# Sparse attention inside a two-layer trunk: which PSUM pool the value products use, where 1/8 is multiplied in, and when the last merge is transposed

## The chip, the cores and the metric

The kernel runs on one NeuronCore of one Trainium2 chip. The metric is the device time of one execution in microseconds (us), the median of three runs.

## What is computed

Two layers. Each is a half-step SwiGLU FFN, then a token-mixing block of three gated branches, then another half-step SwiGLU FFN, each with RMSNorm before and after and with shift, scale and gate from a conditioning vector. There are 256 tokens of width 1024. Only the second branch of the mixing block, the attention, is touched, and the step that merges the branches. The reference, cut to those:

```python
scale = HEAD_DIM ** -0.5                     # 1/8
def query_block(i):                          # 64 queries at a time; 8 heads in 2 groups
    ...
    s = jnp.einsum('bghqd,bgnd->bghqn', qn, kc)
    p_cmp = masked_softmax(s, cmp_end[None, :] <= t[:, None], scale)
    o_cmp = jnp.einsum('bghqn,bgnd->bghqd', p_cmp, vc)
    ...
    p = masked_softmax(s, m_slc, scale)      # selected keys (here: all causal ones)
    o_slc = ...
    p = masked_softmax(s, m_win, scale)      # window keys
    o_win = ...
    return gc[..., 0:1] * o_cmp + gc[..., 1:2] * o_slc + gc[..., 2:3] * o_win
...
branches = jnp.einsum('bsnw,nwd->bsnd', ys, w_branch)      # ys: gMLP, attention, conv
gates = jax.nn.sigmoid(h @ w_gate).reshape(Bsz, S, N_BRANCH, D_MODEL)
merged = jnp.einsum('bsnd,bsnd->bsd', gates, branches)
return merged @ w_out
```

## The kernel before

Every matrix product is done in three fp32r passes: a weight or an activation is split into a high part (`hi`, a copy on ScalarE) and the rest (`lo`, a subtraction on VectorE), and `mm3` (L169 to L172) issues hi by hi, hi by lo and lo by hi into one PSUM bank. Weights stream from HBM one megabyte at a time; `units` (L157) splits each into two such pairs (L164 on ScalarE, L165 on VectorE).

The tokens lie in two tiles of 128 (`t` = 0 and 1). PSUM has eight banks, dealt out by three pools: `ps_y` with four (`y_tile`), `ps_m` with two (`m_tile`) and `ps_t` with two (`t_tile`, for transposes). A tile takes a bank of its pool and gives it back after its last reader. The framework fixes the order of each engine's instructions when the kernel is built, from the order of the program text and from when it reckons each to be ready, and gives a tile its bank or buffer where that order has its first write. So the order on an engine is not quite that of the text.

In `mixing`, two streams of work are interwoven by hand. One is `bulk` (L511), a generator of the projections and branch products: one step is one `mm3` of 512 columns, eight steps make one token tile of a projection (`cg`, `xt`, `bg`, `v`, `u` and the gates `gt`), four steps one of a branch product (`br`). `chunk_steps` (L491) runs the two token tiles of one such product; it takes both banks from `ps_y` at its start and calls `evac` on each tile when its steps are done. The other stream is the attention: 16 pairs of token tile and head. For each, `scores` (L810) issues two products into an `m_tile` named `sc`, VectorE adds the causal mask (L816), takes the maximum (L818) and multiplies it by -1/8 (L819), ScalarE takes the exponential of both softmaxes with scale 1/8 and that bias (L822), and VectorE and ScalarE normalise (L823 to L826). `weights_t` (L829) transposes the result two heads later, and `values` (L856), for each pair of heads, multiplies with the values into another `m_tile`, named `pv`; its results go to the tiles `yTb` (L875 to L882; `yTb` and the pairs `pT`, `u`, `gp`, `ln`, the queries `qhT` and others share one SBUF pool of 14 buffers). The main loop (L885) calls `scores`, `weights_t` and `values` in turn and takes five or six steps of `bulk` after the first two.

The queries reach the scores through `query_hl` (L696): four transposes into one bank, then for each half of the partitions a high copy on ScalarE (L707) and a rest on VectorE (L708).

At the end, `down` (L927) runs the output product `yo`. For the second token tile it first finishes the last branch product (`rest`), whose result is added into `merged[1]` on VectorE (L606, L608); then `out_steps` does three of the eight k-steps (`OUT_AT = 3`), `merged_t(1, 1)` transposes the merged tile into `mT` (L907, L910, L911), and the other steps follow; those from the fifth on read that `mT`. `finish` (L315) puts the norm of the first token tile before this and the transposes of its result (`modulate`, L285) after it.

Of the kernel before, what the change touches and what calls it, by code (L numbers as in the profile page):

```python
# [9 lines left out]
F32 = mybir.dt.float32  # L10
F32R = mybir.dt.float32r
BF16 = mybir.dt.bfloat16
AF = mybir.ActivationFunctionType
ALU = mybir.AluOpType
AX = mybir.AxisListType
# [16 lines left out]
HOLD_CH = 4  # L32
HOLD_END = 2
OUT_END = 4
OUT_AT = 3
S4 = 14
F1 = 3
F2 = (5, 6)
# [36 lines left out]
def trunk(ctx: ExitStack, tc: tile.TileContext, order, x_in, c_in, wst, smalls, gmws, ng_rows, modb, lnrows, rope_c, mask_c, out):  # L75
# [9 lines left out]
    V, A, G, T = nc.vector, nc.scalar, nc.gpsimd, nc.tensor  # L85

    def s4(name, shape=(P, NT, 512), dt=F32):
        return sp.tile(list(shape), dt, name=name, tag="s4", bufs=S4)

    def s2(name, shape=(P, NT, 256), dt=F32):  # L90
        return sp.tile(list(shape), dt, name=name, tag="s2", bufs=S2)
# [4 lines left out]
    def sm(name, shape, bufs=4):  # L96
        return sp.tile(list(shape), F32, name=name, tag=name, bufs=bufs)

    def y_tile(name, n=2):
        return [ps_y.tile([P, 512], F32, name=name, tag="y") for _ in range(n)]  # L100

    def m_tile(name):
        return ps_m.tile([P, 512], F32, name=name, tag="m")

    def t_tile(name):
        return ps_t.tile([P, 512], F32, name=name, tag="t")
# [193 lines left out]
    def proj_steps(o, t, hT, us, width, kpu=2):  # L300
        n = len(us) * kpu
        for k in range(n):
            hi, lo = us[k // kpu]
            c = (k % kpu) * width
            ts = slice(t * P, (t + 1) * P)
            mm3(o, hT[0][:, k, ts], hT[1][:, k, ts], hi[:, c : c + width], lo[:, c : c + width], k == 0, k == n - 1)
            yield
# [179 lines left out]
    def mixing(l, hT, pend, nxt):  # L487
# [1 line left out]
            return units(("in", l, ((lo_c, n),), 0)) + units(("in", l, ((lo_c, n),), 1))  # L489

        def chunk_steps(evac, us, name, width=512, src=None, kpu=2, ts=range(NT)):  # L491
            for t, o in zip(ts, y_tile(name, len(ts))):
                yield from proj_steps(o[:, :width], t, src or hT, us, width, kpu)
                evac(t, o)

# [15 lines left out]
        def bulk():  # L511
            def run(us, name, evac, hooks, **kw):
                for k, _ in enumerate(chunk_steps(evac, us, name, **kw)):
                    if k in hooks:
                        hooks[k]()
                    yield
# [179 lines left out]
        def query_hl(t):  # L696


            o = s4("qhT", (P, 8, P), F32R)
            pt = t_tile("qht")  # L700
            for i in range(4):
                T.transpose(out=pt[:, i * P : (i + 1) * P], in_=qraw[:, t, 2 * i : 2 * i + 2].rearrange("p a d -> p (a d)"), identity=ident)
            pv = pt.rearrange("p (a q) -> p a q", a=4)
            ov = o.rearrange("p (a i) q -> p a i q", i=2)
            for i in range(2):
                r, s = slice(64 * i, 64 * i + 64), slice(64 - 64 * i, 128 - 64 * i)
                A.activation(ov[r, :, i], pv[r], AF.Copy)  # L707
                V.tensor_tensor(ov[s, :, i], pv[r], ov[r, :, i].bitcast(F32), ALU.subtract)  # L708
            return o

        vd = s4("vd", (P, NT, 4, 2, 64), F32R)
# [22 lines left out]
        fill(F1)  # L734
        key_t(kvc, 1)
        qhT = [query_hl(0), None]


# [31 lines left out]
        po = t_tile("po")  # L770
# [6 lines left out]
        po = t_tile("po")  # L777
# [32 lines left out]
        def scores(t, h):  # L810
            g, nk = h // 4, (t + 1) * P
            sc = m_tile("sc")[:, : 2 * nk].rearrange("p (b n) -> p b n", b=2)
            T.matmul(sc, lhsT=qhT[t][:, h], rhs=khv[:, :, g, :nk], start=True, stop=False)
            T.matmul(sc, lhsT=qhT[t][:, h], rhs=klv[:, :, g, :nk], start=False, stop=True)
            dg = sc[:, :, t * P : nk]
            V.tensor_tensor(dg, dg, mask[:, 0:128].unsqueeze(1).to_broadcast([P, 2, P]), ALU.add)  # L816
            mx, nsum = sm("mx", [P, 2]), sm("nsum", [P, 2])
            V.tensor_reduce(mx, sc, axis=AX.X, op=ALU.max)  # L818
            V.tensor_scalar(mx, mx, -0.125, None, op0=ALU.mult)  # L819
            pr = s2("pr", (P, 2, nk))  # L820
            for br in range(2):
                A.activation(pr[:, br], sc[:, br], AF.Exp, scale=0.125, bias=mx[:, br : br + 1], accum_out=nsum[:, br : br + 1])  # L822
            V.reciprocal(nsum, nsum)  # L823
            V.tensor_tensor(nsum, nsum, sg[:, t, h, 1:3], ALU.mult)
            V.tensor_scalar(pr[:, 0], pr[:, 0], nsum[:, 0:1], None, op0=ALU.mult)
            A.activation(pr[:, 1], pr[:, 1], AF.Copy, scale=nsum[:, 1:2])  # L826
            prs[t, h] = pr
# [28 lines left out]
        def values(t, hp):  # L856

            g, nb = hp // 2, t + 1
            po = m_tile("pv")[:, :256]
            hs = slice(2 * hp, 2 * hp + 2)  # L860
            pT = pTs.pop((t, hp))
            pairs = [(vc, [x[:, hs].rearrange("p h q -> p (h q)") for x in pcs[t]])]
            for n in range(2 * nb):
                br, kt = n // nb, n % nb
                pairs.append((vd[:, kt, 2 * br + g], [x[:, n].rearrange("p h q -> p (h q)") for x in pT]))
            for n, (v, (ph, pl)) in enumerate(pairs):
                if n > 0:
                    T.matmul(po[0:64], lhsT=v[:, 0], rhs=pl, start=False, stop=False)
                T.matmul(po, lhsT=v.rearrange("p a d -> p (a d)"), rhs=ph, start=n == 0, stop=n == 2 * nb)
                if n == 0:  # L870
                    T.matmul(po[0:64], lhsT=v[:, 0], rhs=pl, start=False, stop=False)
            ts = slice(t * P, (t + 1) * P)
            hi, lo = [x[:, hp, ts] for x in yT[1]]
            od = sm("od", [P, P], bufs=2)
            A.activation(hi[0:64], po[0:64, 0:P], AF.Copy)  # L875
            A.activation(od[64:128], po[0:64, P:256], AF.Copy)
            A.activation(od[0:64], po[64:128, 0:P], AF.Copy)
            A.activation(hi[64:128], od[64:128], AF.Copy)
            V.tensor_tensor(lo[0:64], po[0:64, 0:P], hi[0:64].bitcast(F32), ALU.subtract)
            V.tensor_tensor(lo[64:128], od[64:128], hi[64:128].bitcast(F32), ALU.subtract)  # L880
            V.tensor_tensor(lo[0:64], lo[0:64].bitcast(F32), od[0:64], ALU.add)
            V.tensor_tensor(lo[64:128], lo[64:128].bitcast(F32), po[64:128, P:256], ALU.add)  # L882

        heads = [(t, h) for t in range(NT) for h in range(8)]
        for i in range(len(heads) + 4):  # L885
            if i < len(heads):
                t, h = heads[i]
                scores(t, h)
                fill(F2[t])
                if h == 0:  # L890
                    cmp_t(t)
                if (t, h) == (0, 4):
                    qhT[1] = query_hl(1)
            if 0 <= i - LAG < len(heads):
                weights_t(*heads[i - LAG])
                fill(F2[heads[i - LAG][0]])
            j = i - LAG - 1
            if 0 <= j < len(heads) and heads[j][1] % 2 == 1:
                values(heads[j][0], heads[j][1] // 2)
# [4 lines left out]
        def merged_t(n, t):  # L904
            pt = t_tile("mt")
            for i in range(4):
                T.transpose(out=pt[:, i * P : (i + 1) * P], in_=merged[n][:, t, i * P : (i + 1) * P], identity=ident)  # L907
            pv = pt.rearrange("p (a b) -> p a b", a=4)
            hi, lo = [x[:, :, t * P : (t + 1) * P] for x in mT[n]]
            A.activation(hi, pv, AF.Copy, scale=0.5)  # L910
            V.scalar_tensor_tensor(out=lo, in0=pv, scalar=0.5, in1=hi.bitcast(F32), op0=ALU.mult, op1=ALU.subtract)  # L911
# [8 lines left out]
        def out_steps(t, ks):  # L920
            ts = slice(t * P, (t + 1) * P)
            for n, ns in enumerate(halves):
                for k in ks:
                    hi, lo = mT[k // 4]
                    mm3(y[t][n], hi[:, k % 4, ts], lo[:, k % 4, ts], wo[k][0][:, ns], wo[k][1][:, ns], k == 0, k == 7)

        def down(t, part):  # L927
# [5 lines left out]
            elif part == 0:  # L933
                for _ in rest[0]:
                    pass
                y[1] = y_tile("yo")
                out_steps(1, range(OUT_AT))
                merged_t(1, 1)
                out_steps(1, range(OUT_AT, 4))
                out_steps(1, range(4, OUT_END))  # L940
# [104 lines left out]
```

## Time and profile before

| | |
|---|---|
| median of 3 runs | 1291.8 us (1289.95 to 1295.27) |
| the profiled execution's own time | 1292.15 us |
| its span, first to last instruction | 1290.4 us |
| the two attention stretches in it | about 270 to 430 us and 901 to 1061 us |
| mean granted TensorE clock | 0.995 of full |

The span is one execution as the hardware profiler saw it. Each row of a timeline has a start in us, a duration, the engine, the line of the kernel, the operation and its tiles, and in brackets how long the engine had been idle and what ended that. Matmuls are pipelined: a row of 0.39 us is followed by the next after about 0.23 us, so rows overlap, and time lost between two matmuls is best read as the distance of their starts less the usual one.

### The profile page before, as it was taken

How to read it: one execution, taken by the hardware profiler on the slowest of the kernel's cores; microseconds unless marked ns; L12 is line 12 of the kernel's file. 1: busy time of each engine (PE TensorE's matmuls, PEld its weight loads, DVE VectorE, ACT ScalarE, POOL GpSimd, SP SyncE). 2: the span in 40 equal slices, each digit the busy share in tenths (PEclk: the TensorE clock that was granted, in tenths of full speed). 3: DMA queues.
4: the chain of work that ended last, by engine and by line, in shares of the span. 5: the costliest groups of instructions: out<-in, count | busy, mean ns of one | idle time of the engine just before them, and what ended most of it. 6: DMA issues, size and time to landing. Idle time of an engine off the chain costs nothing.

```text
span 1290.4 us, 15916 instructions
## 1 busy us (share of the span) xinstructions
PE 1254.8 (97%) x5922; PEld 1027.5 (80%) x5922; DVE 1028.6 (80%) x1632; ACT 680.9 (53%) x1129; POOL 31.6 (2%) x56
## 2 busy tenths in 40 slices
PE   6999999999999999999999999998999999999998
PEld 4788888778778878888878888887877887888886
DVE  7977997789999699767598767587999996875553
ACT  5454446476565464544465444456666574554442
POOL 1000001000000010000010000000000000100000
PEclk8999999999999999999999999999999999999999
DMA  8966885665466548767559767367535763684540
GB/s 328 362 234 248 325 325 193 228 236 186 173 264 238 224 180 326 283 240 292 196 180 350 276 252 272 141 236 285 191 133 224 293 264 132 260 308 170 184 168 33
DMA packets 43904, 304.30 MB, mean 236 GB/s; under 512 B 5169, under 2 KB 5425, under 8 KB 8498
## 3 DMA queue, kind: packets, MB, share of 16 engines
q1 hardware_dynamic: 43634, 303.26, 62.6%
q8 instruction: 46, 0.75, 0.2%
q14 instruction: 32, 0.26, 0.1%
q0 software_dynamic: 192, 0.02, 0.0%
HBM read 302.21 MB, written 1.05 MB: 235 GB/s over the span
## 4 chain that ended last, share of the span: by engine, by line
PE 75%; DVE 12%; ACT 5%; issue 4%; DMA 2%; POOL 1%; DVEq 0%; SPq 0%; POOLq 0%; ACTq 0%
PE gu L172 11%; PE gu L170 11%; PE gu L171 11%; PE yf L172 5%; PE yf L170 5%; PE yf L171 5%; DVE lo L165 3%; PE gt L171 3%; PE gt L172 2%; PE gt L170 2%; ACT hi L164 2%; DMA raw<-w_dram 2%; PE hT L363 2%; DVE raw L189 1%; PE xT L285 1%
## 5 line engine op out<-in xcount | busy, mean ns | idle before, releaser
L165 DVE TENSOR_TENSOR lo<-raw,hi 128x1024 fp32r<-128x1024 f32 (+1 forms) x416 | 495.9, 1210 | 104.4 <-ACT hi L164 100.9
L164 ACT ACTIVATE hi<-raw 128x1024 fp32r<-128x1024 f32 (+1 forms) x416 | 424.9, 1049 | 225.3 <-DMA raw<-w_dram 110.8
L170 PE MATMUL gu<-hi,hT 128*128 128x512 f32 x704 | 278.9, 397 | 4.3 <-ACT hT L412 4.3
L171 PE MATMUL gu<-lo,hT 128*128 128x512 f32 x704 | 275.5, 391 | 1.5 <-DVE lo L165 1.5
L172 PE MATMUL gu<-hi,hT 128*128 128x512 f32 x704 | 275.7, 392 | 0.0
L170 PEld LDWEIGHTS gu<-hi,hT 128*128 128x128 f32 x704 | 132.8, 189 | 31.9 <-ACT hT L412 4.5
L172 PEld LDWEIGHTS gu<-hi,hT 128*128 128x128 f32 x704 | 132.7, 189 | 29.7 <-DVE hT L413 0.7
L171 PEld LDWEIGHTS gu<-lo,hT 128*128 128x128 f32 x704 | 132.9, 189 | 28.9 <-DVE lo L165 2.4
L170 PE MATMUL yf<-hi,hid 128*128 128x512 f32 x352 | 137.6, 391 | 0.0
L171 PE MATMUL yf<-lo,hid 128*128 128x512 f32 x352 | 137.2, 390 | 0.0
L172 PE MATMUL yf<-hi,hid 128*128 128x512 f32 x352 | 137.0, 389 | 0.0
L355 ACT ACTIVATE ht<-gu 128x256 f32<-128x256 f32 x88 | 33.5, 384 | 159.4 <-PE gu L172 159.3
L189 DVE SCALAR_TENSOR_TENSOR raw<-raw,crow 128x1024 f32<-128x1024 f32 x96 | 115.2, 1217 | 2.4 <-DMA raw<-w_dram 1.9
L356 DVE SCALAR_TENSOR_TENSOR ht<-ht,gu 128x256 f32<-128x256 f32 x88 | 36.3, 416 | 60.7 <-ACT ht L355 60.6
L170 PE MATMUL gt<-hi,hT 128*128 128x512 f32 x192 | 76.3, 401 | 0.8 <-ACT th L598 0.8
L172 PEld LDWEIGHTS yf<-hi,hid 128*128 128x128 f32 x352 | 66.1, 188 | 13.7
L171 PE MATMUL gt<-lo,hT 128*128 128x512 f32 x192 | 75.7, 396 | 1.2 <-DVE lo L165 1.1
L171 PEld LDWEIGHTS yf<-lo,hid 128*128 128x128 f32 x352 | 66.1, 188 | 13.5
L170 PEld LDWEIGHTS yf<-hi,hid 128*128 128x128 f32 x352 | 66.1, 188 | 13.5
L172 PE MATMUL gt<-hi,hT 128*128 128x512 f32 x192 | 75.2, 393 | 0.0
L208 DVE SCALAR_TENSOR_TENSOR acc<-raw,cact,acc 128x1024 f32<-128x1024 f32 x48 | 61.4, 1279 | 1.3 <-DMA raw<-w_dram 0.9
L171 PEld LDWEIGHTS gt<-lo,hT 128*128 128x128 f32 x192 | 36.1, 188 | 10.3 <-DVE lo L165 3.6
(297 smaller groups left out, 1770.6 us busy)
## 6 DMA issues: line engine op xcount, KB each, us to landing
raw<-w_dram SPq DMA_DIRECT2D x276, 1024.0 KB, 4.8
raw<-w_dram SPq DMA_DIRECT2D x4, 816.0 KB, 4.2
gate<-ng_dram SPq DMA_DIRECT2D x6, 512.0 KB, 4.8
raw<-w_dram SPq DMA_DIRECT2D x4, 768.0 KB, 4.6
x<-x_dram SPq DMA_DIRECT2D x2, 512.0 KB, 4.6
ln<-ln_dram SPq DMA_DIRECT2D x2, 512.0 KB, 5.9
ws<-gmws_dram SPq DMA_DIRECT2D x2, 256.0 KB, 5.2
out_dram<-x SPq DMA_DIRECT2D x1, 512.0 KB, 2.6
```

The costliest lines, as they stand in the source:

```text
L164: A.activation(hi[:, :width], src, AF.Copy)
L165: V.tensor_tensor(lo[:, :width], src, hi[:, :width].bitcast(F32), ALU.subtract)
L170: T.matmul(o, lhsT=xh, rhs=wh, start=start, stop=False)
L171: T.matmul(o, lhsT=xh, rhs=wl, start=False, stop=False)
L172: T.matmul(o, lhsT=xl, rhs=wh, start=False, stop=stop)
L189: V.scalar_tensor_tensor(out=raw[:, j * D : (j + 1) * D], in0=raw[:, j * D : (j + 1) * D], scalar=1.0, in1=crow, op0=ALU.mult, op1=ALU.mul ...
L208: V.scalar_tensor_tensor(out=acc, in0=raw[:, u * D : (u + 1) * D], scalar=cact[:, k : k + 1], in1=acc, op0=ALU.mult, op1=ALU.add)
L285: T.transpose(out=pt[:, i * P : (i + 1) * P], in_=xn[:, k * P : (k + 1) * P], identity=ident)
L355: A.activation(h, pm[:, :256], AF.Tanh, scale=0.5)
L356: V.scalar_tensor_tensor(out=h, in0=h, scalar=1.0, in1=pm[:, :256], op0=ALU.add, op1=ALU.mult)
L363: T.transpose(out=pt[:, k * S + t * P : k * S + (t + 1) * P], in_=st[j]["h"][:, t, k * P : (k + 1) * P], identity=ident)
```

## The change

`chunk_steps` takes one bank for each token tile when it comes to it, not two at its start. `values` takes its bank from `ps_y`, not from `ps_m`. `query_hl` multiplies the queries by 1/8 as it splits them (ScalarE by its scale operand, VectorE with one operation of another kind), so the scores come out scaled: the maximum is negated by the reduction itself, the multiplication at L819 goes, and the exponential has no scale. `OUT_AT` becomes 1: the second merge of the second token tile is transposed after one k-step of `yo` and not after three.

```diff
-OUT_AT = 3
+OUT_AT = 1
...
         def chunk_steps(evac, us, name, width=512, src=None, kpu=2, ts=range(NT)):
-            for t, o in zip(ts, y_tile(name, len(ts))):
+            for t in ts:
+                o = y_tile(name, 1)[0]
                 yield from proj_steps(o[:, :width], t, src or hT, us, width, kpu)
                 evac(t, o)
...
                 r, s = slice(64 * i, 64 * i + 64), slice(64 - 64 * i, 128 - 64 * i)
-                A.activation(ov[r, :, i], pv[r], AF.Copy)
-                V.tensor_tensor(ov[s, :, i], pv[r], ov[r, :, i].bitcast(F32), ALU.subtract)
+                A.activation(ov[r, :, i], pv[r], AF.Copy, scale=0.125)
+                V.scalar_tensor_tensor(out=ov[s, :, i], in0=pv[r], scalar=0.125, in1=ov[r, :, i].bitcast(F32), op0=ALU.mult, op1=ALU.subtract)
             return o
...
             mx, nsum = sm("mx", [P, 2]), sm("nsum", [P, 2])
-            V.tensor_reduce(mx, sc, axis=AX.X, op=ALU.max)
-            V.tensor_scalar(mx, mx, -0.125, None, op0=ALU.mult)
+            V.tensor_reduce(mx, sc, axis=AX.X, op=ALU.max, negate=True)
             pr = s2("pr", (P, 2, nk))
             for br in range(2):
-                A.activation(pr[:, br], sc[:, br], AF.Exp, scale=0.125, bias=mx[:, br : br + 1], accum_out=nsum[:, br : br + 1])
+                A.activation(pr[:, br], sc[:, br], AF.Exp, bias=mx[:, br : br + 1], accum_out=nsum[:, br : br + 1])
...
             g, nb = hp // 2, t + 1
-            po = m_tile("pv")[:, :256]
+            po = y_tile("pv", 1)[0][:, :256]
```

## Rows read from the trace of the kernel before

**Rows 1.** The page's first part: busy time of each engine, its share of the span, its instructions.

```profile
PE 1254.8 (97%) x5922; PEld 1027.5 (80%) x5922; DVE 1028.6 (80%) x1632; ACT 680.9 (53%) x1129; POOL 31.6 (2%) x56
```

**Rows 2.** The windows view: for each stretch its length, then the busy time of PE, PEld, DVE, ACT and POOL with instructions, the granted clock, the DMA share and GB/s. The first two rows are of the attention of the first layer, the third is the end of its mixing block, the fourth an FFN, the fifth the start of the attention of the second layer.

```profile
270.00:330.00 60.00, 59.52 (x288) 48.78 (x287) 57.99 (x133) 40.83 (x92) 2.67 (x3) 1.00 0.45 169
330.00:370.00 40.00, 37.99 (x184) 30.30 (x183) 38.49 (x76) 23.61 (x51) 0.00 (x0) 1.00 0.58 212
...
430.00:470.00 40.00, 39.13 (x180) 30.78 (x180) 29.47 (x46) 21.90 (x37) 1.65 (x3) 1.00 0.44 163
560.00:620.00 60.00, 60.00 (x274) 49.62 (x273) 43.89 (x62) 26.73 (x32) 0.00 (x0) 1.00 0.73 276
901.00:961.00 60.00, 59.52 (x289) 48.73 (x288) 57.94 (x132) 40.96 (x92) 2.67 (x3) 1.00 0.44 167
```

**Rows 3.** The timeline of PE, first layer: four products that wait for a bank of `ps_m`, each after the matmul before it.

```profile
323.12 0.39 PE L171 MATMUL gt<-lo,hT 128*128 128x512 f32 x1
323.71 0.36 PE L813 MATMUL sc<-kTh,qhT 128*128 128x256 f32 x1 [0.20 <-DVE yTb L882]
...
325.64 0.39 PE L170 MATMUL gt<-hi,hT 128*128 128x512 f32 x1
326.31 0.47 PE L813 MATMUL sc<-kTh,qhT 128*128 128x512 f32 x1 [0.28 <-ACT hi L164]
...
343.94 0.61 PE L170 MATMUL br<-hi,yTc 128*128 128x512 f32 x2
345.15 0.39 PE L869 MATMUL pv<-pcw,vc 120*128 120x256 f32 x1 [0.59 <-ACT pr L822]
...
358.93 0.39 PE L172 MATMUL br<-hi,yTc 128*128 128x512 f32 x1
359.99 0.50 PE L813 MATMUL sc<-kTh,qhT 128*128 128x512 f32 x1 [0.67 <-ACT pr L822]
```

**Rows 4.** The timelines of PE, ACT and DVE between 300 and 330 us: the first writes of the first two `pv` tiles, of the two tiles of `u` and of the first gate tile, and the reads that hold or free them.

```profile
300.54 0.28 PE L869 MATMUL pv<-pcw,vc 120*128 120x256 f32 x1
306.37 0.39 PE L170 MATMUL u<-hi,hT 128*128 128x512 f32 x1
...
316.47 0.28 PE L869 MATMUL pv<-pcw,vc 120*128 120x256 f32 x1
318.56 0.39 PE L170 MATMUL gt<-hi,hT 128*128 128x512 f32 x1
```

```profile
317.37 0.27 ACT L875 ACTIVATE yTb<-pv 64x128 fp32r<-64x128 f32 x1 [0.23 <-PE pv L869]
...
324.23 1.09 ACT L497 ACTIVATE gp<-u 128x512 f32<-128x512 f32 x2 [2.28 <-PE sc L814]
```

```profile
322.34 0.27 DVE L879 TENSOR_TENSOR yTb<-pv,yTb 64x128 fp32r<-64x128 f32 x1
...
323.28 0.29 DVE L882 TENSOR_TENSOR yTb<-yTb,pv 64x128 fp32r<-64x128 f32 x1
...
325.87 0.29 DVE L882 TENSOR_TENSOR yTb<-yTb,pv 64x128 fp32r<-64x128 f32 x1
...
327.26 0.68 DVE L500 SCALAR_TENSOR_TENSOR u<-gp,u 128x512 f32<-128x512 f32 x1
```

**Rows 5.** The view of the tile `mx` (count, durations in ns as min/median/max; then how long others sat idle until one of them, us and times), and the timeline of DVE around one maximum.

```profile
L819 DVE TENSOR_SCALAR mx<-mx x32: 133/160/170, 271.1 to 1031.8; 128x2 f32<-128x2 f32 x32
  ACT pr L822: 31.8, 14
```

```profile
356.99 0.69 DVE L818 TENSOR_REDUCE mx<-sc 128x2 f32<-128x512 f32 x1
...
358.72 0.16 DVE L819 TENSOR_SCALAR mx<-mx 128x2 f32<-128x2 f32 x1
358.79 1.22 DVE L165 TENSOR_TENSOR lo<-raw,hi 128x1024 fp32r<-128x1024 f32 x1
```

**Rows 6.** The line views of the queries' rest and of a subtraction of the changed kind (both from PSUM): count, durations in ns as min/median/max.

```profile
L708 DVE TENSOR_TENSOR qhT<-qht,qhT x8: 683/689/693, 249.1 to 931.4; 64x512 fp32r<-64x512 f32 x8
```

```profile
L911 DVE SCALAR_TENSOR_TENSOR mT<-mt,mT x8: 681/683/692, 437.2 to 1090.1; 128x512 fp32r<-128x512 f32 x8
```

**Rows 7.** The timelines of PE and DVE at the end of the first mixing block.

```profile
456.13 0.60 PE L907 MATMUL mt<-ident,th 128*128 128x128 f32 x4
...
457.74 0.39 PE L172 MATMUL yo<-hi,mT 128*128 128x512 f32 x1
458.73 0.50 PE L170 MATMUL yo<-hi,mT 128*128 128x512 f32 x1 [0.61 <-ACT mT L910]
...
459.53 0.40 PE L171 MATMUL yo<-lo,mT 128*128 128x512 f32 x1
460.19 0.50 PE L172 MATMUL yo<-hi,mT 128*128 128x512 f32 x1 [0.26 <-DVE mT L911]
```

```profile
451.90 0.68 DVE L608 TENSOR_TENSOR th<-th 128x512 f32<-128x512 f32 x1
```

**Rows 8.** The timeline of PE, first layer: a gate product that waits for a bank of `ps_y`, and one that waits for the rest of a weight, after the matmul before it.

```profile
361.54 0.51 PE L170 MATMUL gt<-hi,hT 128*128 128x512 f32 x1 [0.43 <-ACT th L598]
...
368.06 0.39 PE L170 MATMUL gt<-hi,hT 128*128 128x512 f32 x1
368.76 0.50 PE L171 MATMUL gt<-lo,hT 128*128 128x512 f32 x1 [0.31 <-DVE lo L165]
```

## The prediction

> **What bounds the kernel now.** I read the page's busy times first, then the windows of one mixing block beside an FFN, then the timeline of PE for its gaps, and last who ended each gap. PE is busy for 1254.8 of 1290.4 us [rows 1], so at most some 35 us of idle time are to be had anywhere. In an FFN PE has none: 60.00 of 60.00 [rows 2]. In the attention it lacks 0.48 us in the first 60 us and 2.01 us in the 40 us that follow, and 0.87 us at the end of the block; the second layer's first 60 us give the same 59.52 [rows 2]. The reader is to see beside it that VectorE is full in the same stretches, 57.99 of 60.00 and 38.49 of 40.00 [rows 2]. So PE is the bound, and VectorE sets when banks come back; what PE loses, it loses to single waits, the same in both layers. The change can give back those waits and little more, since it takes no matmul away.
>
> A wait's cost I read from starts, since rows of matmuls overlap: with 512 columns one starts 0.23 us after the other. Four products wait for a bank of the two-bank pool [rows 3]. A score at 323.71 starts 0.59 us after the matmul before it (0.36 lost), one at 326.31 after 0.67 (0.44 lost), the value product at 345.15 after some 0.99 (0.76 lost; the second of the two branch matmuls in that row began at about 344.16), one at 359.99 after 1.06 (0.83 lost). That is 2.39 us in each layer.
>
> **The value products' pool.** The first `pv` is written from 300.54 and read for the last time at 323.57, when L882 ends [rows 4]: it holds one of the two banks for 23 us, and the score at 323.71 is released by that read [rows 3]. With `pv` elsewhere, scores have both banks, and each of the four waits in [rows 3] loses its cause: two are scores behind a `pv`, one is a `pv` behind a score, and the last is a score while a `pv` holds the other bank from 345.15 on. I count all 2.39 us as gained; at worst nothing is, if a score that is issued sooner then waits for VectorE.
>
> The price is in the other pool. At 318.56 the first gate tile starts [rows 4]. With `pv` in its pool, the four banks would then hold the first `pv` (to 323.57), `u` of the first token tile (from 306.37, read to 327.94), `u` of the second (later still), and the second `pv` (from 316.47, read to 326.16) [rows 4]. No other step of `bulk` comes before the gate, so PE would have only attention to do: up to 5.0 us of waiting in each layer, from 318.56 to 323.57. What shortens it: the first read of `u` sat 2.28 us idle until the late score's second product had ended [rows 4], and that score is no longer late; the four reads of `pv` by VectorE need 1.23 us (322.34 to 323.57), and would be done 1.2 us after the copies on ScalarE if they came straight behind them. So the ends are 1.2 and 5.0. I take 2.0, nearer to the lower end, because PE can fill some of it with the scores and transposes that now come sooner, and the queue of VectorE behind them is what the change shortens. It is the weakest term of the sum.
>
> Taking one bank at a time costs nothing by itself: no instruction is added, and a tile gets its bank at its first write in the planned order in any case. It only keeps a second bank from being counted as taken.
>
> By the Trainium skill, page "Perfetto Trace Analysis", section "Identifying Performance Opportunities", gaps that repeat on the engine that should be saturated can mean that there is too little PSUM for the next tile. The trace agrees, with the same gaps in both layers and a bank's reader as the releaser of each. The rule speaks against the change as much as for it, since it adds no bank: by it the shortage would only move to the pool of four, which is the slower rival below.
>
> **Queries by 1/8.** L819 is 32 small operations of 0.16 us, but the next on VectorE starts 0.07 us after one (358.72, 358.79) [rows 5]. So removing them frees 32 x 0.07 = 2.2 us of VectorE, 1.1 in each layer. It also shortens a chain: the maximum of 356.99 ended at 357.68, L819 at 358.88 [rows 5], since a weight's subtraction stood between them; the exponentials sat idle 31.8 us on L819, 14 times [rows 5], and the exponential could start up to 1.2 us sooner. ScalarE is not the bound, so this counts only where PE waits at its end: for the rest of a weight at 368.76, which starts 0.70 us after its neighbour (0.47 lost) [rows 8]. I count that 0.47 us in each layer. By the Trainium skill, page "VectorE: DVE Perf Modes", section "The DRAIN you can't avoid", a following operation that is held starts only when the pipeline is empty; were that so here, the 32 would be worth their full 0.16 us, 5.1 us of VectorE. The row of 0.07 us shows that they are not.
>
> What it adds is nothing: the rest of the queries becomes an operation of the other kind, which takes 683 ns on 512 columns from PSUM where the present one takes 689 [rows 6], eight of them in all. No row shows a reduction that negates: at worst it takes L819's 0.16 us with it, so 16 x 0.16 = 2.6 us of VectorE in each layer, at best nothing; I take nothing, as the reduction is one pass in either case.
>
> **The last merge.** PE transposes it at 456.13 and needs its result at 458.73: it starts 0.99 us after the matmul before it (0.76 lost, ended by L910), and at 460.19 another 0.66 after (0.43 lost, ended by L911) [rows 7]. Together 1.19 us in each layer. Two k-steps of two halves are 12 matmuls; at 0.23 us the transposes go 2.8 us sooner in the text, at the earliest where the first six matmuls of that token tile are done, around 454.8. What they read is ready at 452.58 (L608 ends) [rows 7], so the cover is 2.2 us, and no new wait comes in; if that cover were gone, PE would wait at the transposes for as long as it now waits behind them. On ScalarE the copy L910 then stands ahead of the squares of the first tile's norm, and may hold those back by its own 0.6 us; PE has the other half of `yo`, at 24 matmuls some 5 us, to do meanwhile. I count 1.19 us.
>
> **The sum.** Per layer: -2.39 (bank waits) - 0.47 (weight's rest) - 1.19 (merge) + 2.0 (gate tile) = -2.05; twice, -4.1 us. The profiled execution took 1292.15 us, so 1288.0; the median of the runs lies 0.35 lower, so 1287.7 us.
>
> **Rivals.** 1. All is gained and the banks come back in time: VectorE reads `pv` straight behind ScalarE, the gate tile waits less than 0.8 us. Then up to 2 x (2.39 + 0.47 + 1.19) = 8.1 us go, and with the gate's own bank wait of 361.54 (0.43 idle) [rows 8] 9.0: 1283. For it: the waits have one cause, a `pv` that stands long. Against it: VectorE is full just there [rows 2].
>
> 2. Slower: the four-bank pool becomes the short one. At 318.56 PE waits the whole 5.0 us. Later the `pv` begun at 345.15 takes a bank that the branch product has now, while two gate tiles hold theirs until ScalarE reads them at about 361 [rows 8]: the branch's second tile, 12 matmuls of 0.23, is pushed back by 2.8 us. That is 7.8 us in each layer against 3.6 (banks and merge) gained: +4.2, twice +8.4: 1300. It decides from 6.8 us of new waits in each layer on, for there the kernel is 0.5% slower. For it: the four lifetimes above overlap as they stand. Against it: most of them are long because VectorE is behind, and a PE that waits lets it catch up, so that later waits shrink by as much.
>
> 3. The change does not do what it says: the planned order keeps the scores where they are, because they wait for VectorE anyway. Then the merge alone counts, 2 x 1.19: 1289.4.
>
> **How the numbers follow.** Half a per cent, 6.5 us, is about what a measurement of this kernel can tell from no change. Chances: the forecast, a small gain within it, 0.45; rival 3, 0.07; rival 1, 0.33; rival 2, 0.15. So faster 0.33, same 0.52, slower 0.15. The range runs from rival 1 with all that it can give (1282) into rival 2, to where half of its case is left out (1297). The forecast's own range is 1285.3 to 1291.
>
> **What would show it.** Right: in the profile after, no score waits for L882, and the rows at 323.71 and 359.99 have no counterpart; `yo` no longer waits for L910 or L911 and PE's busy time in the last 40 us of the block rises towards 39.9; the gate tile after `u` shows a gap of 1 to 3 us that a read of `pv` or `u` ends. Wrong: that gap is 4 us or more, or branch tiles wait for a read of `pv` (rival 2); no such gap at all (rival 1); or scores that start as late as before (rival 3). A planner that puts the two streams in another order altogether would make the whole sum wrong.

## The result and the profile after

The changed kernel takes 1309.15 us, the median of 4 runs (1308.05 to 1310.34), against 1292.43 us for the kernel before in the same session (4 runs, 1289.95 to 1295.27). The ratio is 1.0133 with a 95% interval of 1.0117 to 1.0150: 16.7 us slower, where 1287.7 was forecast. The profiled execution took 1309.11 us with a span of 1307.4, so the span shows the loss as well: 17.0 us more than before. All times of the chip below are such medians; ratios go to the runs of the kernel before that were taken beside them.

The lines from `chunk_steps` to the maximum stand one number further down than before (L599 is the gate's tanh, L814 and L815 are the scores, L817 the mask, L819 the maximum); from the exponential (L822) on, the numbers are those of before. In the runs below they shift by one more or less, as a run has the added line and the removed one or not.

The page's first part, after:

```profile
PE 1258.6 (96%) x5922; PEld 1032.5 (79%) x5922; DVE 1026.7 (79%) x1600; ACT 683.5 (52%) x1129; POOL 33.4 (3%) x56
```

PE has the same 5922 instructions as in [rows 1] and a little more busy time (some of it at a lower clock). What is new is idle time. Three rows of the waits of PE, after: line, what ended the wait, us in total, times, the longest.

```profile
PE sc L814 <- ACT pr L822: 15.1, 4, 5.6
...
PE xT L285 <- DVE xn L276: 5.7, 9, 1.3
...
PE gt L170 <- DVE yTb L882: 1.1, 2, 0.5
```

The third row is the gate tile of the forecast, the second belongs to the end of the block (both below). The first names the loss: four scores, two in each layer, wait 15.1 us for an exponential to give back their bank. Before, the longest wait of this kind was 0.67 us [rows 3]. The windows of this place, after (columns as in [rows 2]); the last two rows are of the second layer:

```profile
340.00:355.00 15.00, 15.00 (x70) 12.14 (x68) 14.94 (x29) 6.41 (x18) 0.00 (x0) 1.00 0.62 219
355.00:360.00 5.00, 0.26 (x2) 0.00 (x0) 5.00 (x9) 3.79 (x6) 0.00 (x0) 0.81 1.00 410
360.00:365.00 5.00, 2.29 (x4) 1.00 (x4) 5.00 (x9) 3.88 (x11) 0.00 (x0) 0.50 0.89 338
365.00:370.00 5.00, 4.31 (x15) 3.38 (x15) 3.31 (x7) 2.07 (x4) 0.00 (x0) 0.50 0.73 279
370.00:375.00 5.00, 5.00 (x23) 4.15 (x22) 3.67 (x9) 2.87 (x7) 0.00 (x0) 0.82 0.00 0
...
995.00:1000.00 5.00, 1.46 (x7) 0.88 (x5) 4.90 (x10) 3.28 (x4) 0.00 (x0) 0.98 0.90 341
1000.00:1005.00 5.00, 1.22 (x2) 0.50 (x2) 5.00 (x9) 5.00 (x12) 0.00 (x0) 0.50 0.89 321
```

Up to 355 us PE is full. From there it does four matmuls in ten microseconds (x2 in the first five are the tail of the two before), while VectorE is busy all the time, and then the granted clock is 0.50, the 1.2 GHz level, until about 372. The timeline of PE shows the order of the work at this place, after:

```profile
342.43 0.39 PE L170 MATMUL br<-hi,yTc 128*128 128x512 f32 x1
342.65 0.28 PE L869 MATMUL pv<-pcw,vc 120*128 120x256 f32 x1
...
354.65 0.39 PE L814 MATMUL sc<-kTh,qhT 128*128 128x512 f32 x1
354.87 0.39 PE L815 MATMUL sc<-kTl,qhT 128*128 128x512 f32 x1
360.74 0.80 PE L814 MATMUL sc<-kTh,qhT 128*128 128x512 f32 x1 [5.47 <-ACT pr L822]
361.33 0.63 PE L815 MATMUL sc<-kTl,qhT 128*128 128x512 f32 x1
363.94 0.80 PE L814 MATMUL sc<-kTh,qhT 128*128 128x512 f32 x1 [1.98 <-ACT pr L822]
364.53 0.63 PE L815 MATMUL sc<-kTl,qhT 128*128 128x512 f32 x1
365.85 0.79 PE L170 MATMUL br<-hi,yTc 128*128 128x512 f32 x1 [0.69 <-ACT th L599]
...
369.42 0.41 PE L868 MATMUL pv<-pT,vd 128*64 128x256 f32 x1
```

Read from starts, as in the prediction, PE loses 5.64, 2.38 and 1.09 us at the rows of 360.74, 363.94 and 365.85. At the lower level a matmul of 512 columns starts 0.43 us after the one before it, not 0.23 (four starts from 370.28 to 371.56). Over the whole stretch from 355 to 375 us, the distances of starts less the usual ones add up to 12.9 us; before they add up to 2.8. That is 10.1 us more in the first layer, some 9 of the 12.9 lost in the three waits and most of the rest at the lower clock. Read in the same way from 985 to 1015 us, the second layer gives 11.9 against 2.9, so 9.0 more. Together that is 19.1; the span grew by 17.0, so some 2 us came back elsewhere. One place is in the rows: the first score of the first layer starts at 266.63, before at 269.23, when no `pv` is written yet. `e12_scale_s4_15` below, with `pv` in `ps_m`, has most of this lead (267.33), so the pools do not make it, and `e5_scale_only` has none (269.55); what does make it was not tried.

Two rows of ScalarE tell why the branch product stood still. Its second token tile starts at 365.85, when the gate's tanh has read a `gt` tile and so freed a bank of `ps_y`. The tanh itself, before and after:

```profile
360.90 0.58 ACT L598 ACTIVATE th<-gt 128x512 f32<-128x512 f32 x1
361.65 0.60 ACT L598 ACTIVATE th<-gt 128x512 f32<-128x512 f32 x1
```

```profile
365.19 1.08 ACT L599 ACTIVATE th<-gt 128x512 f32<-128x512 f32 x2 [1.31 <-PE sc L815]
```

After, a score ends the wait of the tanh, though no score has anything to do with a gate. The link is a buffer: in the built program `th` takes one of the 14 four-kilobyte SBUF buffers. Before, it follows `yTc` in its buffer, which is free when the branch's second token tile has been multiplied (358.93 in [rows 3] is the last of it). After, it follows the low part of the keys (`kTl`), which is read until the last score. So the wait goes round: branch tile two needs a bank; the two gate tiles have theirs until `th` gets a buffer; `yTc`, the buffer that would come free, waits for branch tile two. The branch's first tile has the third bank, and `pv`, begun at 342.65 and not gone on with until 369.42, has the fourth. Only the end of all scores opens the ring. The scores in turn pass VectorE, whose timeline, after, shows what stands ahead of the mask L817:

```profile
353.14 1.21 DVE L189 SCALAR_TENSOR_TENSOR raw<-raw,crow 128x1024 f32<-128x1024 f32 x1
...
354.34 1.22 DVE L189 SCALAR_TENSOR_TENSOR raw<-raw,crow 128x1024 f32<-128x1024 f32 x1
...
355.75 2.35 DVE L165 TENSOR_TENSOR lo<-raw,hi 128x1024 fp32r<-128x1024 f32 x2
358.02 0.76 DVE L817 TENSOR_TENSOR sc<-sc,mask 128x256 f32<-128x256 f32 x2
```

The scores issued at 354.19 and 354.65 get their mask at 358.02, behind work on weights (4.8 us of it from 353.14 on).

### The profile page after: what moved, and what is told of

The parts are those of the page before. It is cut to its first block, busy times and chain, and to the rows that moved or that the text cites. A ratio compares the mean times of both kernels' runs of the same rounds, so it can differ in the third digit from the quotient of the medians.

```text
span 1307.4 us, 15914 instructions
## 1 busy us (share of the span) xinstructions
PE 1258.6 (96%) x5922; PEld 1032.5 (79%) x5922; DVE 1026.7 (79%) x1600; ACT 683.5 (52%) x1129; POOL 33.4 (3%) x56
## 4 chain that ended last, share of the span: by engine, by line
PE 81%; DVE 8%; ACT 4%; issue 4%; DMA 2%; POOL 1%; SPq 0%; DVEq 0%; POOLq 0%; ACTq 0%
PE gu L172 12%; PE gu L171 11%; PE gu L170 11%; PE yf L172 5%; PE yf L170 5%; PE yf L171 5%; PE gt L170 3%; PE gt L171 3%; PE gt L172 3%; DVE lo L165 2%; DMA raw<-w_dram 2%; PE br L170 2%; ACT hi L164 1%; PE hT L363 1%; PE br L171 1%
## 5 line engine op out<-in xcount | busy, mean ns | idle before, releaser
L165 DVE TENSOR_TENSOR lo<-raw,hi 128x1024 fp32r<-128x1024 f32 (+1 forms) x416 | 496.4, 1211 | 120.4 <-ACT hi L164 115.5
L170 PEld LDWEIGHTS gt<-hi,hT 128*128 128x128 f32 x192 | 36.1, 188 | 8.4 <-ACT od L877 1.5
```

Of the source, the lines that this page charges most:

```text
L165: V.tensor_tensor(lo[:, :width], src, hi[:, :width].bitcast(F32), ALU.subtract)
L170: T.matmul(o, lhsT=xh, rhs=wh, start=start, stop=False)
```

## Experiments

The theory: a ring of two pools, as above; it needs `pv` in `ps_y` and the four-kilobyte buffers full. Rivals: the queries' scale makes the loss, since it lets the scores run ahead of `bulk`; the earlier merge makes it; or the bank that `pv` takes too early does so by itself, whatever the buffers.

**Each part by itself.** `e1_pv_back`, from the changed kernel:

```diff
-            po = y_tile("pv", 1)[0][:, :256]
+            po = m_tile("pv")[:, :256]
```

> The changed kernel, but with the value products' bank taken from ps_m again (the other three parts of the change stay). Bank theory: the loss of 17 us (1309.2 against 1292.4) is made by one value product that holds the fourth ps_y bank from 342.7 us to 372.7 us, so that the branch's second token tile has none, the gate tiles keep theirs and TensorE runs dry from 355 to 365 us in each layer. Without it the two waits of TensorE at scores for the exponential (5.5 and 2.0 us in the first layer) are gone, the granted clock of the stretch stays above 0.9, and the time is 1284 to 1293. Rival, the queries' scale: it lets the scores run ahead of the bulk, and they then leave TensorE without work whichever pool the values use: the time stays at 1304 to 1310 and the wait at the last scores stays over 4 us.

Measured: 1292.05 us, ratio 0.9987 (0.9971 to 1.0003). The long waits are gone, and the clock is full. In the built program `th` follows `yTc` again, as before. The window and what is left of waits for an exponential:

```profile
355.00:370.00 15.00, 13.50 (x66) 10.52 (x66) 14.26 (x24) 10.62 (x23) 0.00 (x0) 1.00 0.62 224
```

```profile
PE sc L814 <- ACT pr L822: 0.7, 2, 0.5
```

`e2_pool_only`, from the kernel before:

```diff
-            for t, o in zip(ts, y_tile(name, len(ts))):
+            for t in ts:
+                o = y_tile(name, 1)[0]
...
-            po = m_tile("pv")[:, :256]
+            po = y_tile("pv", 1)[0][:, :256]
```

> The kernel before with the two pool edits alone (projection banks taken a token tile at a time, value products in ps_y); no scale of the queries, the last merge as before. Bank theory: the loss is there in full, 1303 to 1312, with a stretch of some 10 us in each layer in which TensorE waits at the last scores, and a granted clock of about 0.5 behind it. Rival, the queries' scale: without it no such wait, and the time is 1288 to 1293. Rival, the earlier merge: likewise 1288 to 1293.

Measured: 1313.51 us, ratio 1.0154 (1.0132 to 1.0175), a little above the range that was expected. PE waits at the last scores again, at three of them in each layer and not two; `th` follows queries in its buffer, which are read until the last score like the keys:

```profile
PE sc L814 <- ACT pr L823: 19.4, 6, 4.7
```

`e5_scale_only`, from the kernel before:

```diff
-                A.activation(ov[r, :, i], pv[r], AF.Copy)
-                V.tensor_tensor(ov[s, :, i], pv[r], ov[r, :, i].bitcast(F32), ALU.subtract)
+                A.activation(ov[r, :, i], pv[r], AF.Copy, scale=0.125)
+                V.scalar_tensor_tensor(out=ov[s, :, i], in0=pv[r], scalar=0.125, in1=ov[r, :, i].bitcast(F32), op0=ALU.mult, op1=ALU.subtract)
...
-            V.tensor_reduce(mx, sc, axis=AX.X, op=ALU.max)
-            V.tensor_scalar(mx, mx, -0.125, None, op0=ALU.mult)
+            V.tensor_reduce(mx, sc, axis=AX.X, op=ALU.max, negate=True)
...
-                A.activation(pr[:, br], sc[:, br], AF.Exp, scale=0.125, bias=mx[:, br : br + 1], accum_out=nsum[:, br : br + 1])
+                A.activation(pr[:, br], sc[:, br], AF.Exp, bias=mx[:, br : br + 1], accum_out=nsum[:, br : br + 1])
```

> The kernel before with the queries' scale alone (1/8 in the copy of the queries, maximum negated in the reduction, no multiplication by -1/8 and no scale in the exponential). Bank theory: 1288 to 1294, no wait of over 3 us at a score. Rival, the queries' scale makes the loss: 1303 to 1312, with TensorE waiting 5 us or more at the last scores of each layer.

Measured: 1289.22 us, ratio 0.9969 (0.9957 to 0.9981). `e6_out_only`, from the kernel before:

```diff
-OUT_AT = 3
+OUT_AT = 1
```

> The kernel before with the last merge's transposes ahead of the output projection's second instead of its fourth unit, alone. The prediction's term: 1.2 us less per layer, 1290. Bank theory: says nothing else, 1289 to 1293. Rival, the earlier merge makes part of the loss, since TensorE then waits at the transposes for the merged tile: 1294 to 1300, with a wait of over 1 us at the transposes of the last merge.

Measured: 1293.67 us, ratio 1.0004 (0.9989 to 1.0018), between the two ranges that were expected. So the pools make the loss, all of it; the scale is a small gain, and the merge is worth nothing. Why the last, the rows of `e6_out_only` show: PE at the end of the block, then VectorE and GpSimd.

```profile
454.31 0.60 PE L907 MATMUL mt<-ident,th 128*128 128x128 f32 x4
461.99 1.06 PE L285 MATMUL xT<-ident,xn 128*128 128x128 f32 x8 [0.59 <-DVE xn L276]
476.70 1.09 PE L285 MATMUL xT<-ident,xn 128*128 128x128 f32 x8 [1.31 <-DVE xn L276]
```

```profile
458.55 0.68 DVE L911 SCALAR_TENSOR_TENSOR mT<-mt,mT 128x512 fp32r<-128x512 f32 x1
460.28 0.14 DVE L245 TENSOR_SCALAR rxv<-ssx 128x1 f32<-128x1 f32 x1
460.53 0.16 DVE L246 SCALAR_TENSOR_TENSOR rxv<-ssx,rxv 128x1 f32<-128x1 f32 x1
461.36 0.88 DVE L276 TENSOR_SCALAR xn<-x,rxr 128x512 f32<-128x512 f32 x2 [0.66 <-POOL rxr L248]
```

```profile
468.45 1.22 DVE L165 TENSOR_TENSOR lo<-raw,hi 128x1024 fp32r<-128x1024 f32 x1
468.61 1.46 POOL L248 TENSOR_TENSOR ryr<-ryv,mhalf 128x1 f32<-128x1 f32 x1 [7.29 <-DVE ryv L246]
```

The same step of the kernel before:

```profile
467.95 0.55 POOL L248 TENSOR_TENSOR ryr<-ryv,mhalf 128x1 f32<-128x1 f32 x1 [7.79 <-DVE ryv L246]
```

The transposes at 454.31 have no wait behind them any more, so the 1.19 us of [rows 7] is gained there. It is lost, and more, at the transposes of the next norm, which start 0.76 us late at 461.99 and 1.47 late at 476.70; before, the first has no such gap and the second one of 0.42. The first stands behind the norm of its token tile, whose steps on VectorE now come after L911. In the chain of the second, GpSimd's power (L248) took 1.46 us, where the kernel before shows 0.55. Spans on GpSimd are rough, but these two come by a rule. In the traces of before, after, `e6_out_only` and `e4_s4_15`, all 26 powers of 1.46 or 1.47 us start 0.16 or 0.17 us after the subtraction L165 on VectorE, and none of those of 0.55 or 0.56 starts while an L165 runs. So with the merge moved, the split of a weight comes just ahead of this power, and the power is longer beside it. No run moved that subtraction alone.

**The ring, or the bank alone.** `e3_cmp_last`, from the changed kernel, was to let `pv` take its bank late:

```diff
-            pairs = [(vc, [x[:, hs].rearrange("p h q -> p (h q)") for x in pcs[t]])]
+            pairs = []
...
+            pairs.append((vc, [x[:, hs].rearrange("p h q -> p (h q)") for x in pcs[t]]))
```

> The changed kernel, but each value product multiplies the compressed keys' pair last instead of first, so that it can take its bank only when its probabilities have been transposed. Theory A, the bank taken 27 us ahead of its use is the cause by itself: the bank is taken after 365 us, the branch's second token tile gets one, the wait at the last scores falls below 2 us a layer, and the time is 1286 to 1296. Theory B, the loss is a ring of two pools, in which the second gate tile's result also needs one of the 14 four-kilobyte buffers: that result now follows the transposed probabilities of the same value product in its buffer, so it still comes after the last score, and the wait stays: 1300 to 1312.

Measured: 1313.93 us, ratio 1.0167 (1.0150 to 1.0184), 2 us above the range of theory B. The timelines of PE and ScalarE:

```profile
358.52 0.39 PE L815 MATMUL sc<-kTl,qhT 128*128 128x512 f32 x1
364.86 0.79 PE L814 MATMUL sc<-kTh,qhT 128*128 128x512 f32 x1 [5.96 <-ACT pr L822]
...
373.70 0.56 PE L870 MATMUL pv<-pT,vd 128*128 128x256 f32 x1
...
375.62 0.77 PE L170 MATMUL br<-hi,yTc 128*128 128x512 f32 x1
```

```profile
374.72 0.60 ACT L599 ACTIVATE th<-gt 128x512 f32<-128x512 f32 x1 [1.34 <-PE pv L869]
```

`pv` now begins at 373.70, and nothing is written to its bank between 346.3 and 373.7 (the built program's banks, with the trace's times). Still branch tile two comes behind it. The order of PE was fixed when the kernel was built, and there the bank is `pv`'s. And `th`, as theory B had it, now waits for a buffer of transposed probabilities, which `pv` frees. So a bank held for 27 us in the hardware's time is not the cause by itself. What is left is that it is dealt to `pv` ahead of the branch, with no buffer for `th` before the last score; the next run tries that.

`e4_s4_15`, from the changed kernel, has one buffer more and pays with two small ones; `e4c_s2_7` only pays.

```diff
-S4 = 14
+S4 = 15
...
-S2 = 9
+S2 = 7
```

> The changed kernel with 15 instead of 14 four-kilobyte buffers, paid with 7 instead of 9 two-kilobyte ones; the banks are shared as in the changed kernel. Theory B (ring of the two pools): the gate's result finds a buffer before the last score, the wait at the last scores is below 2 us a layer and the time is 1284 to 1296. Rival, four ps_y banks are too few for gate, branch and values whatever the buffers: 1303 to 1312 with the waits at the scores as in the changed kernel.

> Control of the run with 15 buffers: the changed kernel with 7 instead of 9 two-kilobyte buffers and nothing else. If these two buffers are free to give, it is at the changed kernel's 1309 within 3 us with the same waits. If they are needed, it is slower, by as much as the run with 15 buffers then carries too.

Measured: 1293.29 us with 15 buffers, ratio 1.0014 (1.0002 to 1.0025), and 1310.63 in the control, ratio 1.0145 (1.0130 to 1.0160). One SBUF buffer is worth the whole loss, with the banks dealt from the same pool of four. In the run with 15 the tanh of the gate is back where it was, and no score waits for an exponential:

```profile
359.89 0.60 ACT L599 ACTIVATE th<-gt 128x512 f32<-128x512 f32 x1
```

The plan moved with the buffer: `pv` begins at 353.73 and not at 342.65. But in the built program the four banks still hold the same four tiles ahead of the branch's second one (two gate tiles, its first tile, `pv`). `th` follows transposed probabilities, which `pv` has read by 359.85, and branch tile two starts when that tanh ends:

```profile
353.73 0.28 PE L869 MATMUL pv<-pcw,vc 120*128 120x256 f32 x1
...
360.54 0.50 PE L170 MATMUL br<-hi,yTc 128*128 128x512 f32 x1
```

So the ring is broken at the buffer, with `pv` still ahead of the branch. Whether a fifth bank would break it as well was not tried. What PE waits for in place of the scores:

```profile
PE gt L171 <- DVE lo L165: 3.0, 2, 1.5
PE pt L837 <- DVE yTa L594: 2.8, 2, 1.4
```

`e9_pairs`, from the changed kernel, takes both banks of a projection at once again:

```diff
-            for t in ts:
-                o = y_tile(name, 1)[0]
+            for t, o in zip(ts, y_tile(name, len(ts))):
```

> The changed kernel with the projections' two banks taken together again, as before the change; value products in ps_y, the queries' scale and the earlier merge stay. If the values' place in the pool makes the loss alone: 1306 to 1312, waits at the last scores as in the changed kernel. If taking the banks one at a time is needed for it (a value product slips in between the two token tiles): 1285 to 1296, because the branch then takes both of its banks before the value product.

Measured: 1310.93 us, ratio 1.0145 (1.0130 to 1.0160), with the waits of the changed kernel:

```profile
PE sc L813 <- ACT pr L821: 15.1, 4, 5.6
```

With the values in `ps_y`, one bank at a time or two makes no difference.

**In search of a version that beats both.** `e10_s4_15_out3`, from the run with 15 buffers:

```diff
-OUT_AT = 1
+OUT_AT = 3
```

> The changed kernel with 15 four-kilobyte and 7 two-kilobyte buffers, and the last merge transposed where it was before the change. If the earlier merge gives back at the transposes of the next norm what it gains at the output product (as the traces of the run with 15 buffers and of the earlier merge alone suggest), this is 1 to 3 us below the run with 15 buffers: 1290 to 1292. If the earlier merge gains its 1.2 us a layer here, it is 2 us above: 1295 to 1296.

`e11_scale_out2`, from the scale alone:

```diff
-OUT_AT = 3
+OUT_AT = 2
```

> The kernel before with the queries' scale and with the last merge's transposes ahead of the output projection's third unit. If the cost of the earlier merge is that its result comes ahead of the norm of the next block on ScalarE and VectorE, half the step gives half of the effect or none: 1288.5 to 1291, against 1289.2 for the scale alone. If a step of one unit is early enough to hide the merge and late enough to leave the norm alone, it gains up to 1.2 us a layer: 1286.5 to 1288.

`e12_scale_s4_15`, from the scale alone:

```diff
-S4 = 14
+S4 = 15
...
-S2 = 9
+S2 = 7
```

> The kernel before with the queries' scale, 15 four-kilobyte and 7 two-kilobyte buffers; value products in ps_m. It tells whether the spare buffer is worth something by itself. If it only breaks the ring that the shared pool makes, there is nothing to break here: 1288 to 1291. If the stretch is short of these buffers in any case, 1284 to 1287. If the two smaller buffers are needed: 1291 to 1294.

Measured, in this order: 1290.95 us (ratio 0.9992, 0.9980 to 1.0003), 1290.63 (0.9982, 0.9970 to 0.9993) and 1290.00 (0.9982, 0.9972 to 0.9991). The earlier merge costs 2.3 us in the run with 15 buffers (1293.29 against 1290.95, ratios 1.0014 and 0.9992, each to its own runs of before; the intervals just touch). `e1_pv_back`, which has the earlier merge and one bank at a time beside the scale, lies 2.8 us above `e5_scale_only`, which has the scale alone. Half the step is no gain, and the spare buffer alone is none. The first and the last of the three differ by the two pool edits alone: with the ring broken, the value products' place in `ps_y` is no gain (1.0 us more at the median, with intervals that overlap). The scale by itself stays the fastest, 0.3% below the kernel before; it is nominally ahead of these three, but their intervals overlap with its own.

## Why the prediction was wrong

**The step that failed.** It is the price in the other pool. The sum had one term for it, the gate tile behind `u` (+2.0). That a `pv` begun in the forties takes the bank of the branch's second tile was seen, but only as a part of rival 2: the sum put it at nothing, and the rival priced it at 2.8 us. It measured 10.1 us in the first layer and 9.0 in the second. The terms one by one:

**What bounds the kernel.** Right: PE is the bound and VectorE sets when banks come back. The run with 15 buffers shows it best.

**The four bank waits, -2.39 us a layer.** That these waits would go was right, the gain was not there. In the run with 15 buffers no score waits for a reader of `pv` or for an exponential, as forecast. But PE waits 5.8 us in all (3.0 and 2.8, two rows above) for VectorE, where before the first of these was 1.1 and the second none of note: 4.7 us came where 4.8 us of bank waits went. `e10_s4_15_out3` against `e12_scale_s4_15` (1290.95 and 1290.00) says the same of the time: no gain. VectorE is busy for 67.54 of the 70 us from 300 to 370 there and for 67.64 in the kernel before. An explanation that fits, though no run shows it by itself: scores that come sooner put their work into a full queue, and something else in it comes later. The text had this as the worst case of the term ("at worst nothing is") and counted the best one.

**The gate tile behind `u`, +2.0.** Right in kind, too large: after, it starts 0.70 us late at 317.05, ended by L882, and a branch tile 0.89 late at 332.00; together 1.6 in the first layer. In the second only the gate tile is late (at 958.95, by 0.70 us again).

**One bank at a time, nothing.** Right, as far as `e9_pairs` shows it, in the changed kernel.

**Queries by 1/8, -0.47 a layer, 0.9 in all.** Right in sign, mis-sized: 3.7 us between medians (0.19 to 0.43% by the interval), worked out from `e5_scale_only`. Its profiled execution was the slowest of its ten (1292.08 us), with the span of before, so no trace here shows where the time comes from. VectorE's busy time is 2.9 us less in it (1028.6 [rows 1] and 1025.7), where 2.2 were worked out. The unknown price was nothing, as taken; the view of the tile `mx` in that run has the negated maximum at 550 ns against 548 without:

```profile
L818 DVE TENSOR_REDUCE mx<-sc x32: 391/550/685, 270.8 to 1029.9; 128x2 f32<-128x256 f32 x16, 128x2 f32<-128x512 f32 x16
  ACT pr L821: 23.6, 12
```

The exponentials sat idle 23.6 us on the maximum; before it was 31.8 on L819 [rows 5].

**The merge, -1.19 a layer.** What failed here: "PE has the other half of `yo`, at 24 matmuls some 5 us, to do meanwhile". The cover was real for the output product, but PE reaches the next norm's transposes sooner by what it gained, and the norm did not become sooner: VectorE and GpSimd, which make it, had their order changed by the same edit. The wait moved there and grew.

**Rival 2, the one that came.** Its second place was right to the instruction: a `pv` begun in the forties (345.15 before, 342.65 after) takes the bank of the branch's second tile while two gate tiles hold theirs. Its price, 2.8 us, was the length of those 12 matmuls. The clause that failed is "until ScalarE reads them at about 361 [rows 8]": it took the gates' release as fixed. It hung on the very tile that was being pushed back, through a buffer of another pool. Measured, the place costs 10.1 us in the first layer, 12.9 less the 2.8 that were lost there before, and 9.0 in the second. The sign that it named, branch tiles that wait for a read of `pv`, is not what the trace has: the branch tile waits 0.69 us for the tanh, and the rest of the loss stands at the scores ahead of it. The sentence against the rival, that a waiting PE lets VectorE catch up, failed as well: VectorE is full through the ten microseconds in which PE waits (5.00 of 5.00 us, twice), most of it with weights (L165), while their products stand behind the scores. And the price of an idle PE itself was left out: the matmuls behind it ran at half the clock.

The rule drawn from the Trainium skill, page "Perfetto Trace Analysis", section "Identifying Performance Opportunities", held in the sense in which the prediction used it, since the shortage moved. The page names SBUF beside PSUM as what may be too small for the next tile; the prediction used only half of that. The runs agree with the other half: one SBUF buffer made 17 us of difference (1310.63 and 1293.29), with no bank added.

**The size of it.** Worked out with these rows, rival 2 is 10.1 and 9.0 us at its second place in the two layers and 1.6 and 0.7 at its first, less what came back: slower by well over its 8.4 us in all, and outside a range that ended half way into it, at 1297. The rival stood at a chance of 0.15, and its 1300 was still 9 us short.

## What to carry to other kernels

Before a tile is moved to another pool, follow for each tile of that pool what must happen before its reader can run, buffers of every other pool included: a bank that is freed by an operation whose output needs a buffer, which is freed by a product that needs a bank, is a ring, and its price is not the displaced work but the time until something from outside opens it. In the profile, the sign is a releaser that has nothing to do with the waiting tile's data. And a wait taken from PE in a stretch where another engine is full need not be a gain: here 4.8 us of waits went and 4.7 us of others came.

## What the runs showed of the hardware

The granted clock was 1.00 until PE had been idle; with 0.26 us of work from 355 to 360 us it was 0.81 in those five, then 0.50 (the 1.2 GHz level) from 360 to 370, where PE worked for 2.29 and 4.31 us of each five, and 0.82 from 370 to 375 under full work. In the second layer it was 0.98 from 995 to 1000 us, with PE busy for 1.46, and 0.50 from 1000 to 1005, with PE busy for 1.22. What the clock costs by itself, apart from the wait ahead of it, was not measured by an experiment; an estimate from starts is some 3 to 4 of the 12.9 us (12.9 less the 9.1 of the three waits).

GpSimd's power of one column took 0.55 or 0.56 us, and 1.46 or 1.47 where it started while VectorE was at the 128x1024 subtraction of two SBUF tiles (L165), in all four traces read for it.
